# First block's opening: the indexer query weights loaded between the tiles of x, and two projections that follow the normalised input slice by slice

## The chip, the cores and the metric

The kernel runs on one core of one Trainium2 chip. Its engines are TensorE (PE in the profile, with PEld for its weight loads), VectorE (DVE), ScalarE (ACT), GpSimd (POOL) and SyncE (SP), which here only issues transfers. The metric is the device time of one execution in microseconds.

## The reference

Two decoder layers of a first block, then one layer of a second block, for one sequence of 512 tokens and 1024 features, in float32. A layer of the first block begins so:

```
h = rms_norm(x, norm1[l])
proj = h @ w_in[l]
(a_cq, a_ckv, a_kr, b_q, b_k, b_v, c_q, c_k, c_v, c_qi, c_ki, c_w,
 d_q, d_k, d_v, d_f) = split_cols(proj)
```

Four groups of attention heads follow. Group A goes through low-rank projections of `a_cq` and `a_ckv`, B is a sliding window, C keeps for each query the 128 keys that an indexer scores highest (`c_qi`, `c_ki`, `c_w`), D has forget gates (`d_f`). Then come an output projection and a squared-ReLU feed-forward part. The factor `rsqrt(mean(x*x) + eps)` of the norm is one number per token.

## The kernel before

Activations stand with features on the 128 partitions and the 512 tokens along the row, so x is eight tiles (`xT`, d = 0 to 7). Each product of the first block is made three times in a reduced float32 form: a value is split into a rounded part and a remainder, and `gemm` adds hi·hi, hi·lo and lo·hi. A projection of 128 columns is 24 matmuls of 512 tokens (8 slices, 3 products), all into one PSUM tile with the tag `g`, of which there are three. The norm's factor isn't in h: `fold` multiplies x by the gain and splits it (ScalarE `hh`, L181, then VectorE `hl`, L182), and the factor, `rstd`, is multiplied in where a product leaves PSUM (`evac`, L455).

**The opening.** `xin_load` (L108) loads x as eight tiles of 256 KB, in turn from SyncE's queue and ScalarE's. `load_x` transposes each on TensorE (four 128x128 transposes, L243), copies it out of PSUM on VectorE (L244), and calls `prep_norm`: the two halves of `fold`, a square on ScalarE (L189, L192) and an addition to `ssq` on GpSimd (L193).

**The first products** are steps of `attn`, in an order written out as a string that starts `qi misc rstd Aq Ak qi_rope small score:0 Dp:0 A2`. `proj` takes a raw weight tile, splits it (`split`: `whi` on ScalarE, L132, `wlo` on VectorE, L135, or on GpSimd, L137, after the list `los`) and calls `gemm`. `e_qi` makes two such projections from one load of 1 MB (the query of the indexer, two halves of each head's rotation), `e_misc` one from four narrow pieces, `e_rstd` makes `rstd` from `ssq` with matmuls of ones (L200, L213), `e_Aq` the two of `a_cq`, `e_Ak` that of `a_ckv`. `e_qi_rope` turns qi on VectorE and GpSimd and sends it through memory, `e_small` does the same for the indexer's key (`kr`), `e_score` makes the scores from both (`is`, L557). `Dp:0` is two further projections, whose PSUM tiles stay full until after `A2`. `A2` normalises the low-rank parts of group A and makes their second projections one by one: each result is written to the one `g` tile that is free and evacuated by VectorE (qr, L455 and rotation L306 to L310; then qn, kn, qn, kn) before the next is begun; the values of group A (L682) end it.

**Who sets the order.** A scheduler gives each engine one fixed list by priority, with its own idea of durations. `issue_after(x)` puts what is traced inside behind x on x's engine; `behind(n, m)` does this with matmul m of projection n. Each engine executes its list in order, and so does each queue of transfers. `spill_x` writes the eight `xT` tiles to memory (L227) for later; the pool they lie in, `xin`, is closed afterwards and its space is used again by the tiles of `attn`.

Of the kernel before, what the change touches and what calls it, by code (L numbers as in the profile page):

```python
# [12 lines left out]
F32 = mybir.dt.float32  # L13
# [6 lines left out]
P = 128  # L20
# [21 lines left out]
         "X:7 F:7 F:8 F:9 Dw Y F:10 F:11 F:12 F:13 F:14")  # L42
TURNS = "hlhll"


class Kernel:
# [56 lines left out]
    def xin_load(self):  # L103

        self.xn = []
        for d in range(KD):
            t = self.xinp.tile([P, NB, P], F32, name=f"xn{d}")
            (self.nc.sync if d % 2 == 0 else self.nc.scalar).dma_start(t, self.I["x"][0][:, d * P:(d + 1) * P].rearrange("(b p) c -> p b c", p=P))  # L108
            self.xn.append(t)


    def raw(self, src, nk, ncols):

        t = self.glb.tile([P, 2048], F32, name=self.nm("raw"), tag="raw", bufs=self.raw_bufs)
        v = t[:, :nk * ncols].rearrange("p (k c) -> p k c", k=nk)
        old = self.tc.cur_priority
        self.tc.cur_priority = old - self.rp
        srcs = src if isinstance(src, list) else [src]
        c = ncols // len(srcs)
        for i, s in enumerate(srcs):  # L120
            self.nc.sync.dma_start(v[:, :, i * c:(i + 1) * c], s.rearrange("(k p) c -> p k c", p=P))
        self.tc.cur_priority = old
        return v
# [51 lines left out]

    def fold(self, x, g, d):
# [57 lines left out]
    def load_x(self, xp, first=False, ssq=None):  # L234
# [176 lines left out]
    def attn(self, l, hs, ssq, xin, xout):  # L411
# [33 lines left out]
        def pairsel(raw, r, which, nh):  # L445

            src = raw.rearrange("p k (h t r) -> p t k h r", t=2, r=r)[:, which]
            return [(lambda t: t.rearrange("p k (h r) -> p k h r", r=r), src)]

# [16 lines left out]

        def e_qi():
            raw = raw_in(O_QI)
            with ExitStack() as c:
                for g in self.gates if l == 0 else ():  # L470
                    c.enter_context(self.tc.issue_after(g))
                S["qi"] = proj(pairsel(raw, 16, 0, 8)), proj(pairsel(raw, 16, 1, 8))

        def e_misc():
            rm = self.glb.tile([P, 2048], F32, name=self.nm("rawm"), tag="raw", bufs=self.raw_bufs)
            rm = rm[:, :KD * P].rearrange("p (k c) -> p k c", k=KD)
            nc.gpsimd.memset(rm[:, :, 64:], 0.0)
            for off, n, at in ((O_KR, 32, 0), (O_KI, 32, 32), (O_CW, 8, 64), (O_DF, 4, 96)):
                nc.sync.dma_start(rm[:, :, at:at + n], w_in[:, off:off + n].rearrange("(k p) c -> p k c", p=P))
            s4 = rm[:, :, 0:64].rearrange("p k (s t r) -> p t k s r", s=2, t=2)  # L480
            parts = [(lambda t, i=i: t[:, :, 32 * i:32 * i + 32].rearrange("p k (s r) -> p k s r", s=2), s4[:, i])
                     for i in range(2)]
            parts.append((lambda t: t[:, :, 64:128], rm[:, :, 64:128]))
            S["misc"] = proj(parts)
# [133 lines left out]
        def e_Aq():  # L618
            raw = raw_in(O_CQ)
            S["cq"] = [proj([(full, raw[:, :, j * P:(j + 1) * P])]) for j in range(2)]  # L620
# [1226 lines left out]
    def build(self, start=None):  # L1847
# [91 lines left out]
```

## Time and profile before

| | |
|---|---|
| time, median of 3 runs | 2100.69 us (2099.3 to 2103.05) |
| time of the profiled execution | 2106.34 us |
| its span, first to last instruction | 2104.5 us |
| TensorE busy | 2000.0 us (95%) |
| VectorE, ScalarE, GpSimd busy | 1313.0, 983.7, 335.8 us |
| mean granted TensorE clock | 0.979 of full |

The profiled execution is 5.65 us above the median of the runs. All times in the rows below count from the start of its span. A busy share is the share of the span in which the engine had an instruction; matmuls overlap, so the time between two starts says more than the duration in a row.

### The profile page before, as it was taken

The numbers are of one execution on the slowest core, as the hardware profiler recorded it, in microseconds if no ns is written. First come the engines' busy times: TensorE is split into PE (matmuls) and PEld (weight loads), VectorE is DVE, ScalarE is ACT, GpSimd is POOL, SyncE is SP. The second block draws the span as 40 slices with busy tenths as digits, with TensorE's granted clock in tenths as the row PEclk, the third lists the DMA queues.
The fourth block names the chain that finished last, engine by engine and source line by source line (L and its number), as shares of the span: only waits on it lengthen the run. The fifth ranks groups of instructions, "written<-read, shape, count | busy, mean of one in ns | idle before, by whom it ended". The sixth has DMA issues, their size and how long they took to land.

```text
span 2104.5 us, 27631 instructions
## 1 busy us (share of the span) xinstructions
PE 2000.0 (95%) x10185; PEld 1593.2 (76%) x10185; DVE 1313.0 (62%) x2403; ACT 983.7 (47%) x1799; POOL 335.8 (16%) x270
## 2 busy tenths in 40 slices
PE   7999999999999999999999998999998989989898
PEld 6776778888888776778888887786776777767786
DVE  6588765444436588856666555784585684595564
ACT  4558454233214457654223323654564655555331
POOL 6236220000005236220000001201111112010000
PEclk9999999999999999999999999998999999999999
DMA  6341443233215332354444432343142242243862
GB/s 195 106 118 59 140 132 120 86 119 109 87 61 141 92 108 73 114 161 156 140 132 130 159 120 72 89 125 85 46 128 66 82 119 68 93 133 98 270 215 90
DMA packets 230648, 243.98 MB, mean 116 GB/s; under 512 B 43771, under 2 KB 186026, under 8 KB 230514
## 3 DMA queue, kind: packets, MB, share of 16 engines
q1 hardware_dynamic: 227826, 240.13, 36.7%
q10 hardware_dynamic: 2688, 2.10, 0.3%
q8 instruction: 80, 1.31, 0.3%
q14 instruction: 54, 0.44, 0.1%
HBM read 203.93 MB, written 31.04 MB: 112 GB/s over the span
## 4 chain that ended last, share of the span: by engine, by line
PE 69%; DVE 15%; ACT 6%; DMA 5%; issue 3%; POOL 2%; SPq 1%; DVEq 0%; ACTq 0%; POOLq 0%
PE g L163 17%; PE g L165 17%; PE g L167 17%; PE oT L343 2%; DVE wlo L135 2%; PE pt L334 2%; DVE X L1365 1%; DMA raw<-in_w_in_dram 1%; DVE pr L1363 1%; ACT whi L132 1%; PE S L714 1%; PE l L1247 1%; DVE y L1232 1%; DMA raw<-in_w_out_dram 1%; PE oT L1599 1%
## 5 line engine op out<-in xcount | busy, mean ns | idle before, releaser
L163 PE MATMUL g<-hh,whi 128*128 128x512 f32 (+1 forms) x1392 | 550.1, 396 | 10.8 <-DVE xT L952 5.9
L167 PE MATMUL g<-hh,wlo 128*128 128x512 f32 (+1 forms) x1392 | 550.1, 396 | 3.4 <-DVE wlo L135 3.4
L165 PE MATMUL g<-hl,whi 128*128 128x512 f32 (+1 forms) x1392 | 551.2, 397 | 0.0
L132 ACT ACTIVATE whi<-raw 128x1024 fp32r<-128x1024 f32 (+2 forms) x222 | 222.8, 1013 | 334.7 <-PE g L165 285.5
L163 PEld LDWEIGHTS g<-hh,whi 128*128 128x128 f32 x1392 | 263.7, 190 | 68.5 <-issue 12.9
L167 PEld LDWEIGHTS g<-hh,wlo 128*128 128x128 f32 x1392 | 264.1, 190 | 60.1 <-issue 5.3
L165 PEld LDWEIGHTS g<-hl,whi 128*128 128x128 f32 x1392 | 263.8, 190 | 55.6 <-issue 4.2
L135 DVE TENSOR_TENSOR wlo<-raw,whi 128x1024 fp32r<-128x1024 f32 (+2 forms) x178 | 218.1, 1234 | 81.0 <-ACT whi L132 74.8
L137 POOL TENSOR_TENSOR wlo<-raw,whi 128x1024 fp32r<-128x1024 f32 x44 | 107.8, 2450 | 742.3 <-ACT whi L132 724.4
L163 PE MATMUL g<-sh,dh 128*128 128x512 f32 (+1 forms) x544 | 205.5, 378 | 1.0 <-DVE xT L952 1.0
L165 PE MATMUL g<-sl,dh 128*128 128x512 f32 (+1 forms) x544 | 205.5, 378 | 0.0
L167 PE MATMUL g<-sh,dl 128*128 128x512 f32 (+1 forms) x544 | 204.8, 378 | 0.0
L132 ACT ACTIVATE dh<-raw 128x1024 fp32r<-128x1024 f32 x64 | 64.8, 1050 | 261.5 <-PE g L165 159.3
L961 DVE TENSOR_TENSOR xT<-xT,g 128x512 f32<-128x512 f32 x120 | 82.3, 685 | 133.5 <-PE g L167 133.3
L165 PEld LDWEIGHTS g<-sl,dh 128*128 128x128 f32 x544 | 102.3, 188 | 20.6 <-issue 1.7
L163 PEld LDWEIGHTS g<-sh,dh 128*128 128x128 f32 x544 | 102.3, 188 | 20.6 <-DVE xT L952 1.4
L167 PEld LDWEIGHTS g<-sh,dl 128*128 128x128 f32 x544 | 102.1, 188 | 19.3 <-DVE dl L135 0.3
L920 DVE SCALAR_TENSOR_TENSOR r<-g,rstd 128x512 f32<-128x512 f32 x64 | 44.0, 691 | 100.0 <-PE g L167 99.5
L135 DVE TENSOR_TENSOR dl<-raw,dh 128x1024 fp32r<-128x1024 f32 x64 | 76.5, 1221 | 29.1 <-ACT dh L132 28.8
L331 ACT ACTIVATE L<-L,mn 128x256 f32<-128x256 f32 (+3 forms) x128 | 68.5, 537 | 17.8 <-DVE mn L330 16.9
L193 POOL TENSOR_TENSOR ssq<-sq,ssq 128x512 f32<-128x512 f32 x35 | 52.9, 1511 | 93.6 <-ACT sq L192 92.4
L343 PE MATMUL oT<-ptsb,V 128*64 128x128 f32 x592 | 64.2, 288 | 0.2
(477 smaller groups left out, 3450.6 us busy)
## 6 DMA issues: line engine op xcount, KB each, us to landing
raw<-in_w_in_dram SPq DMA_DIRECT2D x46, 1024.0 KB
raw<-in_w_up_dram SPq DMA_DIRECT2D x32, 1024.0 KB
raw<-in_w_down_dram SPq DMA_DIRECT2D x32, 1024.0 KB
raw<-in_ada_w_dram SPq DMA_DIRECT2D x12, 1024.0 KB
raw<-in_w_in_dram SPq DMA_DIRECT2D x22, 512.0 KB
raw<-in_w_out_dram SPq DMA_DIRECT2D x32, 256.0 KB
fd<-f SPq DMA_DIRECT2D x30, 256.0 KB
xd<-xT SPq DMA_DIRECT2D x24, 256.0 KB
```

What stands on the lines that cost most here:

```text
L132: nc.scalar.activation(f(hi), src, AF.Copy)
L135: nc.vector.tensor_tensor(f(lw), src, f(hi), ALU.subtract)
L137: nc.gpsimd.tensor_tensor(f(lw), src, f(hi), ALU.subtract)
L163: mm.append(nc.tensor.matmul(ps, wh, ah, start=first and k == 0, stop=False))
L165: mm.append(nc.tensor.matmul(ps, wh, al, start=False, stop=False))
L167: mm.append(nc.tensor.matmul(ps, wl, ah, start=False, stop=last and k == nk - 1))
L193: nc.gpsimd.tensor_tensor(ssq, sq, ssq, ALU.add)
L331: nc.scalar.activation(L[:, :n], L[:, :n], AF.Exp, bias=m, scale=-1.0, accum_out=sm[:, hh, i:i + 1])
L334: nc.tensor.transpose(pt[:, jj * P:(jj + 1) * P], L[:, jj * P:(jj + 1) * P], self.ident)
L343: nc.tensor.matmul(oT[hh * 64:(hh + 1) * 64, i * P:(i + 1) * P], V(hh, j0 + jj), pts[hh][:, jj * P:(jj + 1) * P], start=jj == 0, stop=jj = ...
L920: nc.vector.scalar_tensor_tensor(r, ps, 0.0, rstd, ALU.max, ALU.mult)
L961: nc.vector.tensor_tensor(x, x, ps, ALU.add)
```

## The change

The four parts, all in the first layer of the first block:

- **Loads.** SyncE's queue brings x's tile 0, then the qi weights in two halves of 512 KB, then x's tile 6 and the four misc pieces; ScalarE's queue brings the other six tiles of x. The `a_cq` weights, then the constants, then the eight stores of `spill_x` are placed behind these.
- **Products.** The two qi projections move out of `e_qi` into `load_x`: as soon as slice d of h is made, its six matmuls are traced. They go to the two PSUM tiles with the tag `s`, which otherwise hold scores; the transposes with even d use `g` tiles instead. The weights are split in halves of four slices, all remainders on VectorE (`los[:4] = 'v'` takes the entries of qi, misc and the first `a_cq` half, of which three were GpSimd's). `hh` reads the transposed tile from PSUM instead of `xT`.
- **Norm sums.** The squares of slices 0 to 3 are traced four slices later, those of 4 to 7 after all of h.
- **Order.** The string becomes `qi misc Aq rstd` in this layer, with the ones-matmuls behind matmul 4 of projection 3, the first of `a_cq`.

```
     def load_x(self, xp, first=False, ssq=None):
...
-            ps = self.ps.tile([P, T], F32, name=self.nm("xps"), tag="t" if d % 2 else "s", bufs=2)
+            ps = self.ps.tile([P, T], F32, name=self.nm("xps"), tag="t", bufs=2) if d % 2 else self.gtile("xps")
...
-                self.prep_norm(d, self.vec["norm1"][:, d:d + 1], ssq, hs)
-                if d == 4:
-                    self.gates = self.last_fold
+                hs.append(self.fold(self.xT[d], self.vec["norm1"][:, d:d + 1], d, ps))
+                self.first_products(d, hs)
+                if d >= 4:
+                    self.sumsq_add(ssq, self.xT[d - 4], d - 4)
+        if first:
+            with self.tc.issue_after(self.last_fold):
+                self.misc_w = self.split(misc_parts(self.raw_misc), [P, KD, P])
+            for d in range(KD - 4, KD):
+                self.sumsq_add(ssq, self.xT[d], d)
...
+    def first_products(self, d, hs):
+        if d == 0:
...
+            self.qi = [self.ps.tile([P, T], F32, name=self.nm("g"), tag="s", bufs=2) for _ in range(2)]
+            self.qi_mm = [], []
+        for half, at in enumerate((0, 4)):
+            if d == at:
+                k = slice(4 * half, 4 * half + 4)
+                for which, (hi, lo) in enumerate(self.qi_w):
+                    src = pair_columns(self.raw_qi[:, k], 16, which)
+                    self.split([(lambda t: t[:, k].rearrange("p k (h r) -> p k h r", r=16), src)], None, to=(hi, lo))
+        for k in {0: range(0 + 1), 4: range(4, 4 + 1)}.get(d, [d] if 0 < d < 4 or d > 4 else []):
+            for ps, (hi, lo), mm in zip(self.qi, self.qi_w, self.qi_mm):
+                for i, (w, a) in enumerate(((hi, hs[k][0]), (hi, hs[k][1]), (lo, hs[k][0]))):
+                    mm.append(self.nc.tensor.matmul(ps, w[:, k], a, start=k + i == 0, stop=k + i == KD + 1).ins)
...
         def e_rstd():
-            with behind(1, 1):
+            with behind(*((3, 4) if l == 0 else (1, 1))):
...
-        for s in 'qi misc rstd Aq Ak ...'.split():
+        for s in ('qi misc Aq rstd' if l == 0 else 'qi misc rstd Aq').split() + 'Ak ...'.split():
...
-                    self.spill_x()
-                    self.first_consts()
+                    with self.tc.issue_after(self.loaded):
+                        self.raw_cq = self.raw(self.I["w_in"][0][:, O_CQ:O_CQ + 256], KD, 256, loaded=True)
+                    with self.tc.issue_after(self.loaded):
+                        self.first_consts()
+                        self.spill_x()
```

In the lists below a number behind a name is that of a buffer, and the brackets name the engines or transfer counters (DMAHW) that an instruction waits for. TensorE's list before, where the transposes end and the products begin (`xps` is a transposed tile, `g_274` the first qi projection):

```order
L243 MATMUL xps_189<-ident,xn_100 128x128 x3
L243 MATMUL xps_202<-ident,xn_102 128x128 [waits DMAHW0_49,DVE_49]
L243 MATMUL xps_202<-ident,xn_102 128x128 x3
L163 MATMUL g_274<-hh_119,whi_270 128x512 [waits Activation_49]
L165 MATMUL g_274<-hl_120,whi_270 128x512
L167 MATMUL g_274<-hh_119,wlo_271 128x512 [waits DVE_49]
L163 MATMUL g_274<-hh_130,whi_270 128x512
```

The same place after the change (`g_136` and `g_137` are now the two qi projections, `xn_93` is x's tile 5):

```order
L283 MATMUL xps_217<-ident,xn_93 128x128 [waits DMAHW6_49,Activation_49]
L283 MATMUL xps_217<-ident,xn_93 128x128 x2
L313 MATMUL g_136<-hh_128,whi_132 128x512 [waits Activation_49]
L313 MATMUL g_136<-hl_129,whi_132 128x512 [waits DVE_49]
L313 MATMUL g_137<-hh_128,whi_134 128x512 [waits Activation_49]
L313 MATMUL g_137<-hl_129,whi_134 128x512
L283 MATMUL xps_217<-ident,xn_93 128x128
L313 MATMUL g_136<-hh_128,wlo_133 128x512 [waits DVE_49]
L313 MATMUL g_136<-hh_154,whi_132 128x512
L313 MATMUL g_136<-hl_155,whi_132 128x512
```

The products now begin before the transposes of tile 5 are over, and all 48 qi matmuls stand among those of tiles 5 to 7; before, the first of them stood behind the last transpose.

TensorE's list before, where group A's second projections begin (`g_586`, `g_615` are Dp:0, `g_697` is qr's):

```order
L167 MATMUL g_586<-hh_208,wlo_583 128x512
L163 MATMUL g_615<-hh_119,whi_611 128x512
L163 MATMUL g_697<-lat_642,whi_681 128x512 [waits DVE_49]
L165 MATMUL g_697<-lat_642,whi_681 128x512 [waits DVE_49]
L167 MATMUL g_697<-lat_642,wlo_682 128x512 [waits DVE_49]
L163 MATMUL g_697<-lat_648,whi_681 128x512
L165 MATMUL g_697<-lat_648,whi_681 128x512
L167 MATMUL g_697<-lat_648,wlo_682 128x512
L165 MATMUL g_615<-hl_120,whi_611 128x512
L167 MATMUL g_615<-hh_119,wlo_612 128x512
L163 MATMUL g_615<-hh_130,whi_611 128x512
L165 MATMUL g_615<-hl_131,whi_611 128x512
```

The same place after the change, a few matmuls behind the end of Dp:0 (`g_702` is qr's, `g_719` the next, `is` the scores, `ssp` and `ssn` the norm of group A's parts):

```order
L208 MATMUL g_702<-lat_647,wlo_687 128x512
L619 MATMUL is_569<-ki_538,qi_548 128x256 [waits Activation_49]
L204 MATMUL g_702<-lat_653,whi_686 128x512
L240 MATMUL ssp_663<-lt_645,ones 128x512 [waits PE_49,Activation_49]
L619 MATMUL is_574<-ki_538,qi_548 128x384 [waits Activation_49]
L619 MATMUL is_579<-ki_538,qi_548 128x512 [waits Activation_49]
L240 MATMUL ssp_663<-lt_651,ones 128x512 [waits Activation_49]
L206 MATMUL g_702<-lat_653,whi_686 128x512 [waits DVE_49]
L208 MATMUL g_702<-lat_653,wlo_687 128x512
L240 MATMUL ssp_670<-lt_657,ones 128x512 [waits PE_49,Activation_49]
L253 MATMUL ssn_676<-ones,lt_657 128x1 x4
L204 MATMUL g_719<-lat_647,whi_686 128x512 [waits DVE_49]
```

All 48 matmuls of Dp:0 now stand ahead of the first score matmul and of group A's second projections. Before, two of them did, and the other 46 stood among the scores and these projections.

SyncE's queue before (`xd` is the spilled x, `rawm` the misc weights):

```order
L282 DMA bf<-in_fox_b_f_dram 4x1 [waits DMAHW6_49]
L227 DMA xd_215<-xT_104 128x512 [waits DMAHW7_49,DVE_49]
L227 DMA xd_215<-xT_105 128x512 [waits DMAHW0_49,DVE_49]
L479 DMA rawm_328<-in_w_in_dram 128x8x32 [waits DMAHW1_49]
L227 DMA xd_215<-xT_106 128x512 [waits DMAHW2_49,DVE_49]
L227 DMA xd_215<-xT_107 128x512 [waits DMAHW3_49,DVE_49]
L479 DMA rawm_328<-in_w_in_dram 128x8x32 [waits DMAHW4_49]
L227 DMA xd_215<-xT_108 128x512 [waits DMAHW5_49,DVE_49]
```

SyncE's queue after, from the load of the norms' gains (`vrow_296`) to the first spill (`raw_450` is the weight of `a_ckv`):

```order
L107 DMA vrow_296<-in_mla_q_norm_dram 4x128 [waits DMAHW4_49,PE_49,Pool_49]
L107 DMA vrow_296<-in_mla_kv_norm_dram 2x128 [waits DMAHW5_49]
L160 DMA raw_450<-in_w_in_dram 128x8x128 [waits DMAHW6_49,DVE_49]
L107 DMA vrow_296<-in_norm_dram 16x128 [waits DMAHW7_49]
L107 DMA vrow_296<-in_final_norm_dram 8x128 [waits DMAHW0_49]
L107 DMA vrow_296<-in_norm_w_dram 8x128 [waits DMAHW1_49]
L107 DMA vrow_296<-in_c_dram 8x128 [waits DMAHW2_49]
L107 DMA vrow_296<-in_ada_b_dram 24x128 [waits DMAHW3_49]
L107 DMA vrow_296<-in_dn_norm_w_dram 1x128 [waits DMAHW4_49]
L346 DMA bf<-in_fox_b_f_dram 4x1 [waits DMAHW5_49]
L267 DMA xd_332<-xT_113 128x512 [waits DMAHW6_49]
```

Each spill used to wait only for its own copy on VectorE and stood among the other transfers of the opening; now all eight stand behind the weights of `a_ckv`, whose transfer waits for VectorE to be done with the misc weights.

## Rows read from the trace of the kernel before

**Rows 1.** Windows of 20 us: engines' busy time, PEclk the granted TensorE clock.

```profile
0.00:20.00 20.00, 9.40 (x38) 7.37 (x39) 14.24 (x18) 13.44 (x21) 13.44 (x22) 0.84 0.95 282
...
20.00:40.00 20.00, 20.00 (x84) 16.07 (x83) 7.26 (x10) 6.06 (x11) 15.36 (x11) 0.90 0.51 147
...
40.00:60.00 20.00, 19.56 (x89) 15.74 (x88) 15.62 (x21) 10.18 (x18) 6.24 (x4) 1.00 0.42 121
...
60.00:80.00 20.00, 18.93 (x78) 13.20 (x77) 11.20 (x21) 9.23 (x18) 1.77 (x1) 1.00 0.55 143
```

**Rows 2.** Timeline of TensorE, 0 to 31 us: start, duration, waits in brackets.

```profile
4.60 1.97 PE L243 MATMUL xps<-ident,xn 128*128 128x128 f32 x8 [1.75 <-DMA xn<-in_x_dram]
...
14.02 0.80 PE L163 MATMUL g<-hh,whi 128*128 128x512 f32 x1 [2.62 <-ACT whi L132]
...
18.60 0.80 PE L167 MATMUL g<-hh,wlo 128*128 128x512 f32 x1 [3.35 <-DVE wlo L135]
...
20.04 0.63 PE L167 MATMUL g<-hh,wlo 128*128 128x512 f32 x1
...
20.47 0.63 PE L163 MATMUL g<-hh,whi 128*128 128x512 f32 x1
...
24.32 0.40 PE L165 MATMUL g<-hl,whi 128*128 128x512 f32 x1
...
24.55 0.40 PE L167 MATMUL g<-hh,wlo 128*128 128x512 f32 x1
...
26.63 1.02 PE L200 MATMUL ssp<-ssq,ones 128*128 128x512 f32 x2
```

**Rows 3.** DMA over 0 to 40 us, one figure per us, the core's 16 engines.

```profile
GB/s 0 12 232 295 346 295 322 347 359 383 382 368 369 389 184 350 281 279 265 175 371 107 7 0 0 85 317 383 358 299 143 16 0 0 0 0 125 383 86 249
```

**Rows 4.** Timeline of ScalarE and VectorE, 0 to 31 us.

```profile
9.99 0.72 ACT L181 ACTIVATE hh<-xT,norm1col 128x512 fp32r<-128x512 f32 x1
...
12.91 1.06 ACT L132 ACTIVATE whi<-raw 128x1024 fp32r<-128x1024 f32 x1
...
7.23 0.75 DVE L182 SCALAR_TENSOR_TENSOR hl<-xT,norm1col,hh 128x512 fp32r<-128x512 f32 x1
...
9.88 1.17 DVE L182 SCALAR_TENSOR_TENSOR hl<-xT,norm1col,hh 128x512 fp32r<-128x512 f32 x1
...
18.47 3.46 DVE L182 SCALAR_TENSOR_TENSOR hl<-xT,norm1col,hh 128x512 fp32r<-128x512 f32 x2
...
30.67 0.69 DVE L294 TENSOR_TENSOR ra<-g,cosr 128x512 f32<-128x512 f32 x1 [8.74 <-POOL cosr L492]
```

**Rows 5.** Timeline of GpSimd, 0 to 31 us.

```profile
8.93 12.44 POOL L193 TENSOR_TENSOR ssq<-sq,ssq 128x512 f32<-128x512 f32 x7 [5.53 <-ACT sq L192]
```

**Rows 6.** Timeline of VectorE, 36 to 60 us.

```profile
39.21 0.69 DVE L507 TENSOR_TENSOR misc<-g,rstd 128x512 f32<-128x512 f32 x1 [1.63 <-PE g L167]
...
45.02 0.68 DVE L310 TENSOR_TENSOR kr<-ra,rb 32x512 f32<-32x512 f32 x1
```

**Rows 7.** Timeline of TensorE, 55 to 80 us.

```profile
56.87 0.56 PE L557 MATMUL is<-ki,qi 96*128 96x256 f32 x2 [0.44 <-POOL qi L551]
...
69.46 0.50 PE L163 MATMUL g<-lat,whi 128*128 128x512 f32 x1
...
73.86 0.47 PE L163 MATMUL g<-lat,whi 128*128 128x512 f32 x1 [0.20 <-DVE qn L455]
...
79.92 0.36 PE L682 MATMUL g<-whi,lat 128*128 128x256 f32 x1 [0.87 <-DVE kn L455]
```

**Rows 8.** Timeline of VectorE, 66 to 82 us.

```profile
68.72 0.69 DVE L455 TENSOR_TENSOR qr__142_704<-g,rsq 128x512 f32<-128x512 f32 x1 [0.64 <-PE g L167]
...
73.02 0.69 DVE L455 TENSOR_TENSOR qn<-g,rsq 128x512 f32<-128x512 f32 x1
...
79.08 0.69 DVE L455 TENSOR_TENSOR kn<-g,rsk 128x512 f32<-128x512 f32 x1 [1.05 <-PE g L167]
```

**Rows 9.** Timeline of TensorE, 125 to 136 us.

```profile
134.67 0.58 PE L714 MATMUL S<-ah,ah 96*128 96x256 f32 x1 [2.70 <-DVE mn L330]
```

More of the change, by code (lines that the diff above doesn't have):

```diff
@@ L43, with pair_columns, misc_parts @@
 TURNS = "hlhll"
+def pair_columns(raw, r, which):
+    return raw.rearrange("p k (h t r) -> p t k h r", t=2, r=r)[:, which]
+def misc_parts(rm):
+    s4 = rm[:, :, 0:64].rearrange("p k (s t r) -> p t k s r", s=2, t=2)
+    parts = [(lambda t, i=i: t[:, :, 32 * i:32 * i + 32].rearrange("p k (s r) -> p k s r", s=2), s4[:, i])
+             for i in range(2)]
+    parts.append((lambda t: t[:, :, 64:128], rm[:, :, 64:128]))
+    return parts
 class Kernel:
@@ L103, in xin_load, with load, load_misc, raw @@
     def xin_load(self):
-        self.xn = []
-        for d in range(KD):
[L107 to L112, printed above, removed]
+        nc = self.nc
+        self.xn = [self.xinp.tile([P, NB, P], F32, name=f"xn{d}") for d in range(KD)]
+        def load(d, eng):
+            i = eng.dma_start(self.xn[d], self.I["x"][0][:, d * P:(d + 1) * P].rearrange("(b p) c -> p b c", p=P)).ins
+            if eng is nc.sync:
+                self.loaded = i
+        rq, rm = (self.glb.tile([P, 2048], F32, name=self.nm("raw"), tag="raw", bufs=self.raw_bufs) for _ in range(2))
+        rq = self.raw_qi = rq.rearrange("p (k c) -> p k c", k=KD)
+        rm = self.raw_misc = rm[:, :KD * P].rearrange("p (k c) -> p k c", k=KD)
+        nc.gpsimd.memset(rm[:, :, 64:], 0.0)
+        w_in = self.I["w_in"][0]
+        load(0, nc.sync)
+        for half in range(2):
+            with self.tc.issue_after(self.loaded):
+                self.loaded = nc.sync.dma_start(rq[:, 4 * half:4 * half + 4], w_in[half * T:half * T + T, O_QI:O_QI + 256]
+                                                .rearrange("(k p) c -> p k c", p=P)).ins
+        with self.tc.issue_after(self.loaded):
+            load(6, nc.sync)
+        for d in range(KD):
+            if d not in (0, 6):
+                load(d, nc.scalar)
+        with self.tc.issue_after(self.loaded):
+            self.load_misc(rm, w_in)
+    def load_misc(self, rm, w_in):
+        for off, n, at in ((O_KR, 32, 0), (O_KI, 32, 32), (O_CW, 8, 64), (O_DF, 4, 96)):
+            self.loaded = self.nc.sync.dma_start(rm[:, :, at:at + n],
+                                                 w_in[:, off:off + n].rearrange("(k p) c -> p k c", p=P)).ins
+    def raw(self, src, nk, ncols, loaded=False):
         t = self.glb.tile([P, 2048], F32, name=self.nm("raw"), tag="raw", bufs=self.raw_bufs)
@@ L467, in e_qi @@
         def e_qi():
+            if l == 0:
+                S["qi"] = self.qi
+                mms.extend(self.qi_mm)
+                los[:4] = 'v'
+                return
             raw = raw_in(O_QI)
[L469 to L472, printed above, removed]
+            S["qi"] = proj(pairsel(raw, 16, 0, 8)), proj(pairsel(raw, 16, 1, 8))
         def e_misc():
[L475 to L484, printed above, removed]
+            rm = self.raw_misc
+            if l:
+                rm = self.glb.tile([P, 2048], F32, name=self.nm("rawm"), tag="raw", bufs=self.raw_bufs)
+                rm = rm[:, :KD * P].rearrange("p (k c) -> p k c", k=KD)
+                nc.gpsimd.memset(rm[:, :, 64:], 0.0)
+                self.load_misc(rm, w_in)
+            with self.tc.issue_after(mms[-1][-1]):
+                S["misc"] = proj(misc_parts(rm), wts=self.misc_w if l == 0 else None)
         def e_rstd():
-            with behind(1, 1):
+            with behind(*((3, 4) if l == 0 else (1, 1))):
                 S["rstd"] = rstd = self.rstd_rep([ssq], D, "rstd")
```

27 lines of the change are left out of this document (15 added, 12 removed).

## The prediction

> **What bounds the kernel now.** I read the windows first. TensorE is busy in all but a few per cent of the span, so a change pays if it takes idle time or slow clock from TensorE and no other place gives it back. In the first 20 us it is busy for 9.40 us, so idle for 10.60; the next 60 us hold 0.00, 0.44 and 1.07 us of idle time [rows 1]. The opening is where this change acts, and there is something to win.
>
> TensorE's timeline says what the 10.60 us are. The first transposes start at 4.60, when x's first tile has landed, and the change can't move that. Then two waits: 2.62 us until the first qi weights are rounded (14.02), and 3.35 until their remainders are made (18.60) [rows 2]. Behind them the clock is at its lower level: two starts are 0.43 us apart at 20.04 and 0.23 at 24.32 [rows 2]. From 18.60 to about 24.1 that is some 12 matmuls at 0.20 us too much, 2.4 us. Together the opening loses 13.0 us, of which 4.3 are the first wait for x.
>
> The DMA row shows why the qi weights come late: they are the last of 3.1 MB (2.1 of x, 1.05 of weights), the engines move 300 to 380 KB per us from 4 us on, and the sum passes 3.1 MB near 11.5 us [rows 3]; the rounding begins at 12.91 [rows 4]. Any order of loads ends there; only who is last can change.
>
> **The opening after the change.** The qi halves share SyncE's queue with tiles 0 and 6 (1.5 MB), ScalarE's queue brings the other 1.5 MB. If both get half the rate, the first half of the weights is there near 7.2 us, the second near 10, x's tile 5 near 10 and tiles 6 and 7 near 11.5. So TensorE has products from about 10.5 us on, between transposes. What paces it then is the making of h. ScalarE rounds a slice in 0.72, a weight of 1024 columns in 1.06 [rows 4], so half of one in about 0.6; VectorE makes `hl` in 0.75 alone and 1.17 beside GpSimd's additions [rows 4], which run without a pause once they begin, seven in 12.44 us [rows 5]. In its list the second weight halves and two squares stand ahead of `hh` of slice 3: 10.0 + 2 x 0.6 + 2 x 0.6 + 0.7 is 13.1. Then VectorE is the chain: hl 3 to 15.0, hl 4 to 16.2, the second qi remainder (some 1.0) to 17.2, the copy of tile 5 (0.7) to 17.9, on which `hh` 5 waits (18.6), hl 5 to 19.8, two copies to 21.2, hl 6 to 22.4, hl 7 to 23.6. Five matmuls of 0.23 come behind: both qi projections are ready near 24.8. TensorE's own work since 4.60, 32 transposes (some 7 us) and 48 matmuls (11.0), fills 18 of those 20.2 us in small pieces, so I expect the clock at its upper level, at no cost; if it falls, the 2.4 us of before are the price.
>
> From there: the misc remainder is now VectorE's, three pieces behind hl 7, and costs a wait of about 0.3; misc 5.5, `a_cq` 11.0 with the norm matmuls in it (1.9: the two matmuls of ones start at 26.63 and the next product at 28.3 now [rows 2], and the constants' transpose), `a_ckv` 5.5, Dp:0 11.0 and one more set of transposes 0.9. TensorE is through with Dp:0 at 24.8 + 0.3 + 35.8, that is 60.9. Before, the first score matmul starts at 56.87 [rows 7] with 46 matmuls of Dp:0 still to do, 10.6 us: the same work would be done at 67.5. The opening wins **6.6 us**.
>
> Is the other side ready at 60.9? The norm sums come at about 32 instead of 26.63, `rstd` at 34.3, its two products on GpSimd at 1.3 each, then four qi products and the key's chain on VectorE. Before, that chain waited 8.74 us for `rstd` [rows 4] and then for misc, and ran from 39.21 to 45.70 [rows 6]; now misc lies ready and the chain ends near 45. From its end to the first score took 11.2 us (45.70 to 56.87); so scores could start at 56 to 58, ahead of TensorE. The later norm sums cost nothing, since 46 matmuls cover them; without that cover they would cost 5 us.
>
> **Where it is given back.** The last thing before the values of group A is the row of second projections through the one free PSUM tile. The rows show it strictly in turn: qr's evacuation starts at 68.72 and ends at 69.4 [rows 8], and the next projection starts at 69.46; qn's starts at 73.02 behind the rotation [rows 8], and the next starts at 73.86; after the last kn (79.08 [rows 8]) the values start at 79.92 [rows 7]. That is 11.2 us, paced by VectorE, in which TensorE has 18 matmuls of its own, 4.1 us. Before, 46 matmuls of Dp:0 stood in this row and among the scores. After, they are spent. From the first score to qr took 11.85 us before (56.87 to 68.72), 23 of Dp:0 in it (5.3), so 6.6 are left: squares and norms on ScalarE that wait for each other. The new row is 60.9 + 6.6 + 11.2 = 78.7. I leave the 11.2 as it is: one remainder of 1.2 us now stands ahead of the last kn, but a few waits of VectorE for products behind Dp:0 matmuls go.
>
> Against 79.92 this is a gain of **1.2 us**: 5.4 of the 6.6 become idle time of TensorE between 61 and 79. Later the lists differ only in small swaps up to the end of the first attention; from its output projection on TensorE's list is the same. One wait there of 2.70 us on VectorE [rows 9] shows the size that such a swap can win or lose. I take nothing for it and 3 us either way for the range. The profiled execution would take 2106.34 - 1.2 = 2105.1; it stands 5.65 above the median of the runs, so the forecast is **2099.5 us**. A measurement of this kernel can tell about 0.2%, 4.2 us.
>
> **Rivals.** *The lead is kept.* If the row of second projections ends as early as TensorE is ahead, the gain is the 6.6 us: 2094.1. For it: VectorE's own operations in that row are only 10 of 0.7, so with all waits gone it takes 7 us and the products that can't hide 2.7, 9.7 in all, and ScalarE's part may also be shorter. Against it: that alone gives 1.5 us; for the rest the row has to begin earlier, and the rows show each step waiting for the last. A gain over 4.2 us needs the values at 75.7.
>
> *VectorE and GpSimd block each other.* All four early remainders move to VectorE beside GpSimd's additions. The last two `hl` before took 3.46 together, 1.73 each [rows 4], not 1.17. At that price five `hl` and two remainders cost some 4 us more, Dp:0 ends at 65, and the row at 83: 2103. The Trainium skill (SBUF — State Buffer, "Who interferes with whom") says that a VectorE instruction with two SBUF inputs and a GpSimd instruction that reads SBUF block each other in full, whichever began first. The 1.17 beside 0.75 agrees that there is a cost, but is far less than a whole addition of 1.78; by the rule taken whole the time would be the 2103.
>
> *The spills come too late (slower).* The tiles of `attn` take the space of x, so the turned qi and misc may not be written before the eight spills have landed. They are now issued behind the weights of `a_ckv`, at some 27 us, and 2.1 MB at 330 KB per us need 6.4: landing near 36, 1.5 after `rstd`. It decides from 40 us on; then each us is one us of the whole. Stores that wait for each other's counters and land at 46 would give 2105.5. Against it: before, none of the eight took part in a wait.
>
> *The change does nothing*, since weights arrive after x anyway: excluded by the bytes above unless ScalarE's queue gets nearly all the rate; it would end near 2101.
>
> **The numbers.** The forecast with the VectorE rival near it and the empty one, within 0.2%: 0.48. The lead kept, or kept by more than half and helped by a later swap: 0.30. Slower by over 0.2%, by spills, blocked VectorE and a bad swap together: 0.22. The range goes from 7 below the forecast (the 6.6 kept) to 6 above (late spills): 2092.5 to 2105.5. The likeliest case alone has 2096.5 to 2102.5.
>
> **What would show it.** In the changed profile: qi products from 10 to 11 us on, the last near 24.8; TensorE without idle time from 25 to 61; the first score near 61; over 4 us of idle time before the values of group A start, and these at 78 to 80. I am wrong if the values start before 76 or after 84, if a wait on the spills shows near 40, or if the difference arises behind 120 us.

## The result and the profile after

The changed kernel takes 2121.62 us (median of 4 runs, 2117.85 to 2122.34), the kernel before 2101.7 beside it: a ratio of 1.0075, 95% interval 1.006 to 1.0089. By the medians it is 19.9 us slower; the ratio stands for 15.8 us, and the two profiled executions differ by 16.0. So the loss is 16 to 20 us. The forecast was 2099.5, and its slow rival ended at 2105.5.

The windows of the changed kernel, with the same columns as [rows 1]:

```profile
0.00:20.00 20.00, 13.65 (x52) 10.82 (x53) 11.66 (x16) 9.76 (x16) 9.18 (x19) 1.00 0.66 173
20.00:40.00 20.00, 19.21 (x88) 14.64 (x87) 10.33 (x13) 9.13 (x17) 4.23 (x4) 1.00 0.69 223
40.00:60.00 20.00, 15.89 (x63) 12.41 (x62) 18.07 (x21) 6.25 (x11) 11.24 (x7) 0.85 0.45 130
60.00:80.00 20.00, 17.89 (x71) 13.33 (x70) 11.63 (x16) 11.58 (x23) 4.03 (x2) 0.93 0.33 96
80.00:100.00 20.00, 15.60 (x57) 11.69 (x57) 8.95 (x11) 6.15 (x9) 5.18 (x3) 0.54 0.36 88
```

The opening improved: TensorE is busy 13.65 us of the first 20 instead of 9.40. The loss lies between 40 and 100 us: 4.1, 2.1 and 4.4 us idle in three windows, and a granted clock of 0.54 in the last, that is, mostly the lower level. TensorE's timeline (columns as in [rows 2]) says where:

```profile
34.44 1.02 PE L240 MATMUL ssp<-ssq,ones 128*128 128x512 f32 x2
...
51.29 0.39 PE L208 MATMUL g<-hh,wlo 128*128 128x512 f32 x1
55.23 0.76 PE L204 MATMUL g<-hh,whi 128*128 128x512 f32 x1 [3.55 <-DVE lt L517]
55.79 0.63 PE L206 MATMUL g<-hl,whi 128*128 128x512 f32 x1
56.21 0.63 PE L208 MATMUL g<-hh,wlo 128*128 128x512 f32 x1
...
57.83 1.11 PE L588 MATMUL mt<-ident,misc 128*128 128x128 f32 x4 [0.56 <-DVE misc L580]
...
69.90 0.45 PE L619 MATMUL is<-ki,qi 96*128 96x256 f32 x2
...
76.47 1.12 PE L240 MATMUL ssp<-lt,ones 128*128 128x512 f32 x2 [2.04 <-ACT lt L697]
...
83.47 0.79 PE L204 MATMUL g<-lat,whi 128*128 128x512 f32 x1 [1.84 <-DVE qn L517]
...
92.25 0.55 PE L744 MATMUL g<-whi,lat 128*128 128x256 f32 x1 [0.87 <-DVE kn L517]
```

At 51.29 the last matmul of `a_ckv` starts; by the prediction's own count (Dp:0 done at 67.5 before, 11.0 long, and 0.9 for `mt`, the transposes of misc) TensorE is then 4.1 us ahead of before. Then Dp:0, the work that was to cover everything, can't begin: it waits 3.55 us for `lt`, the evacuation of `a_cq` or `a_ckv`. These hold all three `g` tiles. Behind the wait the starts are 0.42 us apart, the lower clock, until about 60.5. The first score comes at 69.90 (56.87 in [rows 7]), the values of group A at 92.25 (79.92 in [rows 7]): 12.3 us late. At the eighth residual addition of the first output projection, the end of this layer's attention, it is 13.9 (282.86 against 268.93). So only 1.6 us are lost between 92 and 283 us; the lag behind that (the span is 16.0 longer) was not traced.

VectorE's timeline, then GpSimd's, then that of SyncE's queue, show why `lt` is late:

```profile
40.14 0.69 DVE L569 TENSOR_TENSOR misc<-g,rstd 128x512 f32<-128x512 f32 x1 [4.35 <-DMA xd<-xT]
...
45.36 1.68 DVE L371 TENSOR_TENSOR rb<-misc,sin 32x512 f32<-32x512 f32 x1
47.07 1.67 DVE L372 TENSOR_TENSOR rb<-misc,sin 32x512 f32<-32x512 f32 x1
48.77 1.66 DVE L373 TENSOR_TENSOR kr<-ra,rb 32x512 f32<-32x512 f32 x1
50.46 2.76 DVE L374 TENSOR_TENSOR kr<-ra,rb 32x512 f32<-32x512 f32 x1
53.25 1.23 DVE L176 TENSOR_TENSOR wlo<-raw,whi 128x1024 fp32r<-128x1024 f32 x1
54.40 0.68 DVE L517 TENSOR_TENSOR lt<-g,rstd 128x512 f32<-128x512 f32 x1
```

```profile
40.16 1.29 POOL L554 TENSOR_TENSOR cosr<-cos,rstd 128x512 f32<-128x512 f32 x1 [12.58 <-DMA xd<-xT]
...
44.77 1.73 POOL L364 TENSOR_TENSOR o<-ra,rb 128x512 f32<-128x512 f32 x1
46.83 1.36 POOL L565 TENSOR_TENSOR cosr<-cosr,rstd 128x512 f32<-128x512 f32 x1 [0.34 <-DMA cosr<-in_rope_tab_dram]
48.33 1.55 POOL L565 TENSOR_TENSOR sinr<-sinr,rstd 128x512 f32<-128x512 f32 x1
49.84 2.84 POOL L178 TENSOR_TENSOR wlo<-raw,whi 128x1024 fp32r<-128x1024 f32 x1
```

```profile
28.15 0.41 SPq L160 DMA_DIRECT2D raw<-in_w_in_dram  x1
...
32.88 4.04 SPq L267 DMA_DIRECT2D xd<-xT  x8
```

Three delays in a row. The norm sums come at 34.44, so `rstd` is ready at 36.85. The spills are issued at 32.88 and not landed until 40, and nothing may be written into x's old space before: 3.3 us more. Then the key's rotation takes 7.8 us in its last four steps, which alone take 0.68 each: each runs while GpSimd is busy, and ends half a microsecond behind GpSimd's operation.

The row from the first score to the values took 22.35 us, 4.5 longer than forecast. VectorE's timeline there, then GpSimd's:

```profile
75.93 0.69 DVE L517 TENSOR_TENSOR qr__142_709<-g,rsq 128x512 f32<-128x512 f32 x1
...
78.51 2.75 DVE L372 TENSOR_TENSOR rb<-qr__142_709,sin 64x512 f32<-64x512 f32 x1
...
82.72 0.69 DVE L517 TENSOR_TENSOR qn<-g,rsq 128x512 f32<-128x512 f32 x1
85.21 0.69 DVE L517 TENSOR_TENSOR kn<-g,rsk 128x512 f32<-128x512 f32 x1 [1.80 <-issue]
88.99 0.69 DVE L517 TENSOR_TENSOR qn<-g,rsq 128x512 f32<-128x512 f32 x1 [3.09 <-PE g L208]
...
91.42 0.69 DVE L517 TENSOR_TENSOR kn<-g,rsk 128x512 f32<-128x512 f32 x1 [0.61 <-PE g L208]
```

```profile
77.80 2.92 POOL L178 TENSOR_TENSOR wlo<-raw,whi 128x1024 fp32r<-128x1024 f32 x1 [11.52 <-ACT whi L173]
```

From qr's evacuation to qn's it is 6.79 us, 4.30 before (68.72 to 73.02 in [rows 8]): one rotation step takes 2.75 instead of 0.69 beside GpSimd, and a remainder of 0.43 stands in between. From qn's to the values it is 9.53, 6.90 before: there TensorE's clock is at the lower level (0.50 from 82.7 to 92.25).

### The profile page after: what moved, and what is told of

The parts are those of the page before. It is cut to its first block, busy times and chain, and to the rows that moved or that the text cites. A ratio compares the mean times of both kernels' runs of the same rounds, so it can differ in the third digit from the quotient of the medians.

```text
span 2120.5 us, 27639 instructions
## 1 busy us (share of the span) xinstructions
PE 2008.5 (95%) x10185; PEld 1597.9 (75%) x10185; DVE 1320.6 (62%) x2410; ACT 985.2 (46%) x1801; POOL 328.2 (15%) x265
## 4 chain that ended last, share of the span: by engine, by line
PE 67%; DVE 14%; ACT 6%; DMA 3%; issue 3%; POOL 2%; SPq 1%; DVEq 0%; ACTq 0%; POOLq 0%
PE g L204 17%; PE g L206 17%; PE g L208 17%; PE oT L407 2%; DVE wlo L176 2%; PE pt L398 2%; DVE X L1427 1%; DVE pr L1425 1%; ACT whi L173 1%; PE S L776 1%; PE l L1309 1%; DMA raw<-in_w_out_dram 1%; PE oT L1661 1%; DVE y L1294 1%; DVE y L1295 1%
## 5 line engine op out<-in xcount | busy, mean ns | idle before, releaser
L204 PE MATMUL g<-hh,whi 128*128 128x512 f32 (+2 forms) x1376 | 543.2, 396 | 11.4 <-DVE xT L1014 5.9
L208 PE MATMUL g<-hh,wlo 128*128 128x512 f32 (+1 forms) x1376 | 543.6, 396 | 0.6 <-DVE wlo L176 0.5
L206 PE MATMUL g<-hl,whi 128*128 128x512 f32 (+2 forms) x1376 | 543.4, 396 | 0.0
L173 ACT ACTIVATE whi<-raw 128x1024 fp32r<-128x1024 f32 (+4 forms) x227 | 224.6, 1000 | 336.2 <-PE g L206 288.4
L204 PEld LDWEIGHTS g<-hh,whi 128*128 128x128 f32 (+1 forms) x1376 | 260.6, 189 | 68.4 <-issue 16.8
L206 PEld LDWEIGHTS g<-hl,whi 128*128 128x128 f32 (+1 forms) x1376 | 260.6, 189 | 54.4 <-issue 3.8
L176 DVE TENSOR_TENSOR wlo<-raw,whi 128x1024 fp32r<-128x1024 f32 (+4 forms) x185 | 221.6, 1207 | 86.8 <-ACT whi L173 80.2
L395 ACT ACTIVATE L<-L,mn 128x256 f32<-128x256 f32 (+3 forms) x128 | 68.7, 539 | 15.1 <-DVE mn L394 14.3
L233 POOL TENSOR_TENSOR ssq<-sq,ssq 128x512 f32<-128x512 f32 x35 | 51.5, 1471 | 100.9 <-ACT sq L232 99.9
```

Of the source, the lines that this page charges most:

```text
L173: nc.scalar.activation(f(hi), src, AF.Copy)
L176: nc.vector.tensor_tensor(f(lw), src, f(hi), ALU.subtract)
L204: mm.append(nc.tensor.matmul(ps, wh, ah, start=first and k == 0, stop=False))
L206: mm.append(nc.tensor.matmul(ps, wh, al, start=False, stop=False))
L208: mm.append(nc.tensor.matmul(ps, wl, ah, start=False, stop=last and k == nk - 1))
L233: nc.gpsimd.tensor_tensor(ssq, sq, ssq, ALU.add)
```

## The experiments

The theories: **A**, the chain from the norm's factor to the evacuations `lt` is late, so TensorE has no free PSUM tile for Dp:0, idles and falls to the lower clock; **B**, VectorE being held up beside GpSimd does it alone; **C**, the row of second projections without Dp:0 in it is what costs; **D**, lists behind 100 us matter. Measured, in us (second to fifth column from the one profiled execution of each run):

| run | first `lt` | first score | values of A | 8th addition | ratio to before, 95% |
|---|---|---|---|---|---|
| before | 46.45 | 56.87 | 79.92 | 268.93 | 1 |
| changed | 54.40 | 69.90 | 92.25 | 282.86 | 1.0075 (1.006 to 1.0089) |
| e1 spills early | 50.45 | 68.12 | 86.09 | 283.22 | 1.008 (1.0061 to 1.0099) |
| e2 sums early | 54.84 | 71.52 | 93.20 | 282.15 | 1.0079 (1.0058 to 1.01) |
| e3 both | 47.21 | 65.25 | 83.22 | 279.27 | 1.0053 (1.0031 to 1.0075) |
| e4 GpSimd idle | 53.56 | 65.06 | 87.52 | 276.88 | 1.0039 (1.0023 to 1.0054) |
| e5 e1, `mt` back | 51.89 | 64.52 | 84.16 | 282.34 | 1.0051 (1.0036 to 1.0066) |
| e6 e3, `mt` back | 47.45 | 60.68 | 78.79 | 276.86 | 1.0038 (1.0025 to 1.0052) |
| e7 spills second | 52.47 | 66.32 | 88.81 | 280.33 | 1.005 (1.0035 to 1.0065) |
| e8 Dp:0 held | 47.12 | 60.46 | 82.24 | 273.01 | 1.0015 (0.9999 to 1.0031) |
| e9 store behind | 47.54 | 57.32 | 75.86 | 265.51 | 0.9979 (0.9967 to 0.9992) |
| e10 e9, GpSimd idle | 46.61 | 56.76 | 75.28 | 264.57 | 0.9979 (0.9969 to 0.9988) |
| e11 held, both | 47.48 | 56.83 | 75.81 | 266.39 | 0.9982 (0.9969 to 0.9995) |
| e12 before, late spills | 50.54 | 66.85 | 85.42 | 278.04 | 1.0046 (1.0031 to 1.0061) |

The opening is nearly the same code in the changed kernel and in e1 to e11, yet TensorE reaches the remainder of the misc weights between 26.77 us (e4) and 28.47 (e5). So a difference of under 1.7 us between two rows of this table may come from the opening alone.

### e1: the spills back to their place

```
+                    self.spill_x()
                     with self.tc.issue_after(self.loaded):
                         self.raw_cq = ...
...
                         self.first_consts()
-                        self.spill_x()
```

> The eight spills of x go back ahead of the a_cq weights, each waiting only for its own copy; all else as changed. Theory A (the chain from the norm's factor to the evacuation of a_cq and a_ckv is late, TensorE finds no free PSUM tile for Dp:0 at 51.3, idles 3.55 us and falls to half clock): the first write into x's old space comes at about 37 instead of 40.1, the first lt at about 51 instead of 54.4, the wait at 51.3 is under 0.5 us, no half clock from 55 to 60, the values of group A start at 80 to 85 instead of 92.25, time 2107 to 2114. Theory B (the key's rotation on VectorE is slow beside GpSimd, 8.7 us instead of 4.5, and this alone makes the wait): lt moves under 1 us, time 2119 to 2121. Theory C (the row of second projections without Dp:0 in it costs the time whatever comes before it): the wait goes but the values still start at 88 to 90, time 2117 to 2119.

VectorE and TensorE in this run:

```profile
36.17 0.69 DVE L569 TENSOR_TENSOR misc<-g,rstd 128x512 f32<-128x512 f32 x1 [0.88 <-ACT rstd L244]
```

```profile
53.92 1.09 PE L588 MATMUL mt<-ident,misc 128*128 128x128 f32 x4 [6.91 <-issue]
54.66 0.78 PE L208 MATMUL g<-hh,wlo 128*128 128x512 f32 x1
```

The chain did what A said: `misc` 4.0 us earlier, waiting for `rstd` now, `lt` at 50.45. The wait had changed its place: with the spills earlier in its own plan the scheduler had put the transposes of `misc` (`mt`) into `a_ckv`, and TensorE waited there 6.91 us for the scan on VectorE (the running sum of the forget gates, made in `misc`), which ends at 53.8. Even so the values came 6.2 us earlier than in the changed kernel. The time did not move, since the stretch from the values to the eighth addition became 6.5 us longer (197.1 instead of 190.6), which is theory D and is taken up below. So this run says nothing of A's time.

### e2 and e3: the norm sums early, alone and with the spills

```
-            with behind(*((3, 4) if l == 0 else (1, 1))):
+            with behind(*((2, 2) if l == 0 else (1, 1))):
...
-        ('qi misc Aq rstd' if l == 0 else 'qi misc rstd Aq')
+        ('qi misc rstd Aq')
```

> The ones-matmuls go from behind the fifth matmul of a_cq to behind the third of misc; the spills stay late. Theory A with both delays in a row: rstd is ready near 31 instead of 36.85, but what is written into x's old space still waits for the spills until 40, so lt starts at 54 to 54.5 as now and the time is 2120 to 2123. If the place of the norm sums alone were the cause: lt 5 us or more earlier, time 2107 to 2112.

> Both together. Theory A: rstd near 31, the first product with it near 32, lt below 48, no wait of TensorE at 51.3, all of Dp:0 done at 62 to 63, values of group A at 79 to 85, time 2101 to 2108; below the run with early spills alone by 0 to 6 us, since Dp:0 then hides most of what is left. Theory B: over 2112. Theory C: 2115 or more.

Sums alone, on VectorE:

```profile
40.60 0.69 DVE L569 TENSOR_TENSOR misc<-g,rstd 128x512 f32<-128x512 f32 x1 [3.20 <-DMA xd<-xT]
```

As expected: the ones-matmuls ran at 28.54, 5.9 us earlier, and nothing followed, because the spills still held the space. In e3 both delays are gone and `lt` comes 7.2 us earlier than in the changed kernel, but `mt` stood ahead of the last matmul of `a_cq` (a wait of 4.9 us). The values came at 83.22, inside the expected 79 to 85; the time, 2114.03, missed the expected 2108 by 6, and again the stretch behind the values was longer (196.1).

### e4: GpSimd idle beside the key's rotation

```
-                los[:4] = 'v'
+                los[:8] = 'vvvvv'
...
-                nc.gpsimd.tensor_tensor(t, t, S["rstd"], ALU.mult)
+                (nc.gpsimd if l else nc.vector).tensor_tensor(t, t, S["rstd"], ALU.mult)
```

> The changed kernel with the two products of the key's tables and the second remainder of Dp:0 on VectorE instead of GpSimd, so that GpSimd is idle while VectorE rotates the key. All theories: the four rotation steps that took 1.68, 1.67, 1.66 and 2.76 us take 0.68 each. Theory A: the chain still starts at 40.1 and VectorE has 2.6 us more of its own to do, lt starts 1 to 2 us earlier, time 2117 to 2121. Theory B: kr is ready 4 to 5 us earlier and the wait at 51.3 goes, time 2108 to 2113.

```profile
45.74 0.68 DVE L372 TENSOR_TENSOR rb<-misc,sin 32x512 f32<-32x512 f32 x1
46.45 0.68 DVE L373 TENSOR_TENSOR kr<-ra,rb 32x512 f32<-32x512 f32 x1
...
48.37 0.68 DVE L374 TENSOR_TENSOR kr<-ra,rb 32x512 f32<-32x512 f32 x1
```

TensorE:

```profile
53.64 1.08 PE L588 MATMUL mt<-ident,misc 128*128 128x128 f32 x4 [3.39 <-issue]
```

Three steps now take 0.68; the first still took 1.68, beside a GpSimd operation that was left. `kr` is done 4.2 us earlier (1.3 of it because `misc` itself came at 38.80 in this run), `lt` only 0.84, since VectorE does the moved work itself: so far A. The wait of TensorE that was to go by B stayed, 3.39 us instead of 3.55. Yet the values came 4.7 us earlier, and the time, 2111.36, lies where B put it. What gained was not the freed rotation alone: the plan had put `mt` in front of Dp:0, where it shares the one wait, some five matmuls of Dp:0 ran at the lower clock instead of nine, six matmuls of Dp:0 moved behind the first score, and the opening was 1.4 us earlier in this run anyway. The row behind still had a rotation step of 2.72 beside GpSimd. So the step times show what GpSimd does to the rotation; what that costs in the whole while the factor is late, this run can't tell.

### e5, e6, e7: the same with the transposes of misc back in place

`mt` becomes a step of its own, traced behind Dp:0 and held behind its fifth matmul, close to where it stood in the changed kernel (behind the fourth). For this Dp:0 is traced ahead of the first scores. e7 puts the spills directly behind the `a_cq` weights, ahead of the constants.

```
+        def e_mt():
+            with behind(*((6, 4) if l == 0 else (4, 20))):
...
-        Ak qi_rope small score:0 Dp:0 A2
+        Ak qi_rope small Dp:0 mt score:0 A2
```

> As the run with early spills alone, but the transposes of misc (mt), which the scheduler had then moved 13 matmuls ahead into a_ckv, stand again behind the first matmuls of Dp:0, as in the changed kernel. Theory A (late factor, late evacuations, no free PSUM tile): the first lt at 50 to 51, no wait over 0.6 us between 27 and 62, Dp:0 done at 62 to 63, values of group A at 80 to 82 (92.25 in the changed kernel, 79.92 before). Theory B (the idle time belongs to misc's transposes wherever they stand, because the scan on VectorE is late): another wait of 2 us or more on mt. Theory D (what is won until 100 us is lost again by the other lists behind 100 us): time 2113 to 2118 although the values start at 82 or earlier; without D 2102 to 2105.

> As the run with both early, mt in the same late place. Theory A: lt at 47, no wait of TensorE between 28 and 62, first score at 61 to 62, values at 78 to 80, that is where the forecast had them. Theory D: the eighth residual addition of the first output projection (268.93 before, 279.27 with both early) still comes 4 us or more late, time 2106 to 2110; without D 2098 to 2101.

> The changed kernel with the spills directly behind the a_cq weights, ahead of the constants (they were behind them and behind the a_ckv weights), and mt in the changed kernel's place. Theory A: the spills land before 30, the first write into x's space is at 36 to 37, lt at 51, values of group A at 80 to 83. If the constants, now 2.1 MB later, hold the products with the factor instead: first product later than 40, values at 90 or later.

VectorE and TensorE in e6:

```profile
47.45 0.68 DVE L517 TENSOR_TENSOR lt<-g,rstd 128x512 f32<-128x512 f32 x1
```

```profile
60.68 0.56 PE L625 MATMUL is<-ki,qi 96*128 96x256 f32 x2 [0.83 <-POOL qi L619]
...
78.79 0.36 PE L750 MATMUL g<-whi,lat 128*128 128x256 f32 x1 [1.06 <-DVE kn L517]
```

This is the test of A, and up to the values it holds: with the factor's chain early, TensorE works from 28 to 58 us without a wait, the first score comes 9.2 us earlier than in the changed kernel and the values 13.5. In e5 the values came at 84.16 and not by 82: waits of 0.75 and 1.21 were left, and the scores' inputs were ready only at 64.5. In e7 they came at 88.81: the products with the factor waited for the constants until 38.21 instead, `lt` came at 52.47 and TensorE still waited 2.15 us for it. e7 and e6 have the same order of steps, so they are the nearest pair for A: `lt` 5.0 us earlier, the first score 5.6, the values 10.0. In the whole time A is not seen by itself: e6 is still 0.38% slower than before.

D holds as well. e6 is 1.1 us ahead of before at the values and 7.9 behind at the eighth addition; e5 goes from 4.2 to 13.4. That stretch takes 196 to 198 us in e1, e3, e5 and e6 and 189 to 193 in all other runs, 189.0 before and 190.6 in the changed kernel. In these four TensorE is idle in it for 14.3 to 14.4 us instead of 12.0 before, and the mean granted clock is 0.95 to 0.97 instead of 0.97. In e6 its longest waits there are for the softmax's `mn`, 3.94 and 3.21 us, where the changed kernel has 2.46 and 1.33. Which difference of the lists makes them longer stays open.

### e8: Dp:0's second half held back

Both delays gone as in e3, `mt` behind the last matmul of `a_ckv`, and:

```
+                    if l == 0 and p == 0 and j:
+                        c.enter_context(self.tc.issue_after(S["first_is"]))
```

> Both early, and the second half of Dp:0 (24 matmuls) held behind the first score matmul, so that it fills the row of second projections again. Theory C (an empty row gives the lead back): first score at 57 to 59, values at 74 to 77, under 2 us of idle time and no half clock between 55 and 80. If the row is as long with the fillers as without: values at 78 to 80 as in the run without the hold. Theory D: part of it is lost behind 100 us.

The first score did not come at 57 to 59; it waited 3.0 us for its inputs, until 60.46. So these are the next limit, whatever TensorE does. The row took 21.8 us and not less, so this run speaks against C. All runs together say more. The matmuls of Dp:0 between the first score and the values, the time of this row, how much of it lies between qr's evacuation and the first qn's and from there to the values, and the granted clock of the whole row:

| runs | matmuls of Dp:0 in the row | row, us | qr to qn | qn to values | granted clock |
|---|---|---|---|---|---|
| changed, e2, e4, e7 | 0 to 6 | 21.7 to 22.5 | 6.8 to 6.9 | 8.9 to 9.6 | 0.68 to 0.84 |
| e1, e3, e6, e9, e10, e11, e12 | 15 to 26 | 18.0 to 19.0 | 4.8 to 4.9 | 6.9 to 8.1 | 1.00 |
| e5 | 15 | 19.6 | 4.8 | 7.1 | 0.91 |
| e8 | 24 | 21.8 | 4.9 | 8.2 | 0.87 |

An empty row is no shorter but 3 to 4 us longer, and two things make it so. In exactly the four runs with the empty row GpSimd makes a weight remainder of 2.9 us while VectorE rotates qr, and one rotation step takes 2.7 us instead of 0.69: that is the 2.0 us from qr to qn. The rest comes behind qn, where TensorE is at the lower clock. e8 came into its row from the wait of 3.0 us and began at the lower level too: its row is 2.7 us longer than that of e11, the same hold without the wait, up to qr's evacuation. C holds as far as that, and B has a share in it. The lists of these runs differ elsewhere as well, so this is a reading over runs and not a test of one edit; no run takes GpSimd's remainder out of an empty row.

### e9, e10, e11: what holds the scores' inputs

SyncE's queue in e6:

```profile
51.62 0.27 SPq L595 DMA_DIRECT2D cumd<-misc  x1
51.93 0.51 SPq L602 DMA_DIRECT2D kst<-kr  x1
...
53.11 3.15 SPq L615 DMA_DIRECT2D qst<-qd  x6
```

The store `cumd` waits 3.4 us for the scan on VectorE, and the loads of the scores' inputs stand behind it. e9 is e6 with this store traced at the start of `A2`; e10 adds the edit of e4; e11 is e8 with both.

```
+            if l == 0:
+                self.sd.dma_start(S['cumd'], S['cum_rows'])
             gq = self.vec["mla_q_norm"]
```

> As the run with both early and mt in place, and the store of the forget gates' sums (cumd), for which SyncE's queue waited until 51.6 with the loads of the scores' inputs behind it, now stands behind these loads. Theory A': with the factor early the score's inputs are the next limit; their loads are issued from 47 on, ki and qi are ready by 56 to 57 instead of 60.6, the first score comes at 58 to 60 (Dp:0 sets it), values of group A at 76 to 78. If that queue is no limit: first score at 60.5 and values at 78.8 as without. The time also hangs on the lists behind 100 us: 2100 to 2110.

> The same, with the key tables' products and the second remainder of Dp:0 on VectorE. VectorE alone: the key's rotation takes 0.7 a step, kr ready at 43 to 44 instead of 46.3. Theory A': no further gain before 80 us, since Dp:0 ends at 59 and sets the first score; values at 76 to 78. Theory B (VectorE beside GpSimd still holds TensorE): values 2 us or more earlier than in the run without this.

> As the run with the second half of Dp:0 held behind the first score, with the store behind and GpSimd idle beside VectorE: score's inputs by 55, first score at 57 to 58 without the 3.0 us of wait, values at 78 to 80 (82.24 with the hold alone); time 2098 to 2106.

TensorE in e9:

```profile
57.32 0.46 PE L627 MATMUL is<-ki,qi 96*128 96x256 f32 x2
...
75.86 0.36 PE L754 MATMUL g<-whi,lat 128*128 128x256 f32 x1 [1.06 <-DVE kn L517]
```

The first score comes 3.4 us earlier than in e6 and the values 2.9; in all three the values come up to 2.2 us earlier than expected. The lists behind lose 0.3 to 1.6 in these runs instead of 9. Why they lose less there isn't shown. All three are faster than the kernel before, e9 by 0.21% (2099.39 us, interval 0.08 to 0.33%), and by the ratios some 20 us faster than the changed kernel. In e10 the values come only 0.6 us earlier than in e9, no more than its opening does (0.5), and the time is the same: with the factor early the key's rotation beside GpSimd is hidden. Holding Dp:0 back brings nothing more.

### e12: late spills alone, in the kernel before

```
-                    self.spill_x()
                     self.first_consts()
+                    with self.tc.issue_after(self.last_vrow):
+                        self.spill_x()
```

> The kernel before with one part of the change alone: the eight spills behind the constants and, by the queue's order, behind the weights of a_cq and a_ckv. Theory A: the spills land at 32 to 34, the first write into x's old space (cosr, 29.33 before) waits for them, qi's evacuations end 3 us or more later, TensorE waits 2 us or more for a free PSUM tile near 38 to 42, values of group A at 83 to 86 (79.92 before), time 2104 to 2112. If late spills cost nothing while the products go to g tiles: no wait on them, values within 1 us of 79.92.

```profile
38.43 1.28 POOL L492 TENSOR_TENSOR cosr<-cos,rstd 128x512 f32<-128x512 f32 x1 [5.51 <-DMA xd<-xT]
```

`cosr` runs at 38.43 instead of 29.33. TensorE waits 0.9 us for a PSUM tile at 40.02 and 3.1 at `mt`; the values start 5.5 us late and the kernel is 0.46% slower, 9 us. So moving eight stores is worth over half the loss by itself, also without the rest of the change. The spills landed at 38.4 and not at 32 to 34, the tile wait was smaller than expected, the wait at `mt` not expected.

## Why the prediction was wrong

**The opening: right, and mis-sized.** The qi products began at 12.13 (forecast 10 to 11) and ended at 27.06 (24.8); `hl` 7 ended at 25.75 (23.6). TensorE ended `a_ckv` at 51.5; the forecast's terms make it 49.0, so 4.1 of the 6.6 us were won. (The forecast's own sum has a step that its terms don't give: from 13.1 one `hl` of 1.17 ends at 14.3, not at 15.0.)

**"The chain ends near 45 ... The later norm sums cost nothing, since 46 matmuls cover them": this step failed**, in two ways. The chain ended at 53.2: `rstd` 2.5 us later than I said, the spills 3.3, the rotation 5.0 longer than its steps alone; against that the rest of the chain took 2.7 less than I gave it. And the cover was not there. I counted 46 matmuls of Dp:0 as free work, but they need a PSUM tile, and the three `g` tiles were full of `a_cq` and `a_ckv`, which only `rstd` and VectorE, behind that same chain, can empty. Work covers a delay only if it doesn't need the delayed thing. e6 shows the step repaired: with `lt` at 47.45 the wait is gone. Of the 13.5 us between the values forecast (78.7) and measured (92.25), 9.0 are this: Dp:0's end at 69.9 and not 60.9, of them 2.5 from the opening, 3.7 of idle time, 0.6 at `mt` and the rest, 2.2, at the lower clock.

**Late spills: the right rival, with a wrong threshold.** I had them land at 36 and decide from 40 us on (my terms, 27 and 6.4, make 33.4 and not 36). They were issued at 32.88 and not at 27, behind the weights of `a_ckv` (28.15) and the small loads that follow these. They held the chain until 40, and they decide from 36.85 on, when `rstd` is ready, since the chain had no slack left. e2 shows that an early factor gains nothing while they are late, and e12 shows them as a cause by themselves. The wait on them near 40 was one of my signs of being wrong.

**VectorE and GpSimd: dismissed on a misread row.** I took 1.17 beside 0.75 as a mild cost, and priced it in the opening alone. The cost is the rest of whatever GpSimd is doing (below), and it struck the key's rotation, which I had not looked at: 7.8 us for four steps. How much of the loss hangs on that, no run shows by itself.

**The row of second projections, 17.8 forecast and 22.35 measured: the other 4.5 us.** The mechanism stood (nothing is left to fill the row), its size failed. Up to qr's evacuation the row took 6.0 us, 0.6 less than forecast; from there to the values 16.3 instead of the 11.2 that I left as they were. Of these 5.1 us, 2.1 are the rotation step beside GpSimd (2.75 instead of 0.69) and 0.4 the remainder ahead of qn. The other 2.6 lie behind qn, where the clock is lower, which I left out: TensorE came into this part after a wait of 2.04, and from 78.7 on its matmuls start 0.43 us apart instead of 0.23. Of these matmuls 12 stand between one evacuation and the next, some 2.4 us; the other six were over while VectorE still rotated qr. That idle time of TensorE brings the lower clock stood in [rows 2]; I used it for the opening only. That e6 has its values at 78.79 is no proof of my 17.8: its row of 18.1 had 19 matmuls of Dp:0 left in it.

**"I take nothing for the later lists, and 3 us either way": nothing was nearly right here (1.6 us), the bound not.** In e5 and e6 they cost 9 us.

## What to carry to other kernels

Before calling queued work a cover, list what it waits for itself: a buffer that is emptied by the late chain makes the cover wait with it. A store of a buffer whose space is used again is on the path of the first writer of that space; moving it "out of the way" of loads moves it into the way of that writer. Where a scheduler makes the lists, pin the neighbours before reading a one-line experiment: e1 hid a true cause behind a wait that had moved and behind lists that had become slower.

## What the runs showed of the hardware

In these traces a short VectorE operation with both inputs in SBUF that meets a running GpSimd operation ends a fixed time behind it, as if it waited for it rather than ran slower beside it. In the changed kernel the four rotation steps end at 47.04, 48.74, 50.43 and 53.22, and GpSimd's operations at 46.50, 48.19, 49.88 and 52.68: 0.54 to 0.55 us before, each time. GpSimd is held up too: its operation at 44.77 takes 1.73, one of the same shape at 43.51 takes 1.30. `hl` 7 ends at 25.75, 0.55 behind the sixth addition to `ssq`. An evacuation, with one input in PSUM, isn't held: `lt` at 47.45 in e6 takes 0.68 while GpSimd's operation runs from 46.65 to 49.79. The Trainium skill (SBUF — State Buffer, "Who interferes with whom") says that a VectorE instruction with two SBUF inputs contends with a GpSimd instruction that reads SBUF, and that the pair of ports they share is an exclusive lock. The traces agree, in that the step waits for the end of GpSimd's operation; that it then ends 0.54 to 0.55 behind, and not the 0.68 that it takes alone, the page doesn't say.

In the changed kernel the matmuls between 13.1 and 15.5 us start 0.42 us apart, as at the lower level, though the record of the granted clock reads 1.00 there; from 55 to 60 us the same distance goes with 0.50. Why the record differs is open.
